# A hybrid conv and attention layer on one core: the last pair's sums in SBUF, one weight half on VectorE, and four steps moved in time

## The chip, the core and the metric

The kernel runs on one core of one Trainium2 chip. The metric is device microseconds of that core for one execution. The engines are TensorE (PE, with weight loads shown apart as PEld), VectorE (DVE), ScalarE (ACT), GpSimd (POOL) and SyncE (SP, which here issues DMAs only). ACT also issues a few DMAs (its queue is shown as ACTq).

## The reference

S = D = 1024, all in float32. A decoder layer with two branches from one projection:

```
mod = c @ w_ada + b_ada;  shift, scale, gate = split(mod, 3)
h = rmsnorm(x, norm_g) * (1 + scale) + shift
glu_a, glu_b, z_conv, q, k, v, z_att, g_conv, g_att = split(h @ w_in)
u = causal_conv31(glu_a * sigmoid(glu_b)) + conv_b
y_conv = (silu(layernorm(u, conv_ln_g, conv_ln_b)) * silu(z_conv)) @ w_conv_out
att = dilated causal window attention, 3 groups of 8 heads of 64, rope on q and k
y_att = (att * silu(z_att)) @ w_att_out
merged = sigmoid(g_conv) * y_conv + sigmoid(g_att) * y_att
out = rmsnorm(x + gate * (merged @ w_o)) * final_g
```

## The kernel before

**Arithmetic.** A float32 operand is split in a high part (rounded to the type that TensorE takes at full rate, fp32r) and a low part (the rest), and each product is three matmuls: high by high, low by high, high by low (L73 to L75, L616, L276). ACT makes a high half by a copy (`whi`, L57, L462), POOL or DVE the low one by a subtraction (`wlo`, L58, L465). Names: `hh` and `hl` are the halves of h (with the channels on the partitions), `wraw` a weight tile as loaded, `d` a PSUM bank.

**Start.** The first products are those of the values. They run on x times a gain before the full h is known. For the first of eight channel tiles the gain column comes from a modulation product on DVE (L171, L298); then `gained_high(0, half)` (L240, on ACT) makes the high part of x, `v_high(0, half)` (L250, on ACT) that of the weights, and DVE makes the second half of x (L301). PE's first matmuls (L276) take both. Later `scaled(kt)` (L355 to L362) makes h of a channel tile: DVE multiplies by the row of root mean squares (L359), ACT writes the high part and the full h (L361), SP stores it. In the loop at L391 DVE makes the low part of h (L393) and, by `shift(kt)`, the shift column of a later tile (L171, L174).

**The planned stage** (from L426). Units of matmuls are steps; `at(step, rank, fn)` hangs the other engines' work onto a step, by rank (EARLY, COPY, EVICT, HIGH, POST and so on), and what is hung at a step is written out around that step's matmuls. `Raw(step, source)` is a weight load at a step, `Form` its split into halves, `Gated` the eviction of a product with its gate. The layer norm of the conv branch sums squares on DVE (`tot`, L801, L805), then sixteen 1-wide matmuls (L130) turn the totals into column sums, eight small DVE and ACT operations make the scales (`lcols`, L113 to L136), and PE transposes those (L821). Just then PE works on the values: groups of twelve matmuls (L616). The conv branch's output weights (`w_co`, eight tiles) are loaded by `output(step, d)`; each output tile multiplies by a loaded gate (`sgc`, L924), is stored to `cscr` (L930), and a column of the output gate is computed beside it (`gate_sum`, its weights `wada`, L937, by DVE at L171). The columns go to `gscr` (L1115). All these transfers are issued by SP in program order, and an instruction that waits on SP holds those behind it.

**Attention.** Slots of half a projection unit each (from −11) carry a hand-written order for PE, DVE, ACT and SP. POOL is not in it: its order is set by the framework's scheduler. `out_combos(k)`, k = 0 to 3, loads two tiles of `w_o` (`oc`, L1549), combines them by four POOL operations (L1552, L1553, L1555, L1556) and stores them to `tscr` (L1559); its four parts are hung on four slots. POOL also makes the low halves (L58) of the projection's weights. `move_kq` (L1287) moves finished keys and queries (`kqp`) between partitions by DMA; the scores (L1357) read them as `k`, `q` and `ql`. Slot 0 has the first scores.

**The end.** Pairs of row tiles t1 and t2 come out of `merged @ w_o` in four accumulations. For the last pair `last_part(t, n, ps, first)` (L1842 to L1847) multiplies a half of 512 columns by the gate, adds the residual, takes the sum of squares on ACT and multiplies by `final_g`; `out_norm` gives total, root (on ACT) and refinement of the inverse root, and `both_rows` (L1959 to L1970) scales the two tiles and stores them.

Of the kernel before, what the change touches and what calls it, by code (L numbers as in the profile page):

```python
# [8 lines left out]
F32 = mybir.dt.float32  # L9
F32R = mybir.dt.float32r  # L10
I32 = mybir.dt.int32
AF = mybir.ActivationFunctionType
# [4 lines left out]
P = 128  # L17
S = 1024
D = 1024
KT = 8  # L20
# [19 lines left out]
def layer(ctx: ExitStack, tc: tile.TileContext, a, out):  # L40
    nc = tc.nc
# [134 lines left out]
    with sbuf_pool("start") as st, tc.manual_schedule(  # L176
# [6 lines left out]
        wa_t, v_raw, u_raw = {}, [], []  # L183
# [62 lines left out]
        def shift(kt):  # L246
            modulation(kt, scol[:, kt:kt + 1], wa_t[kt], wa_t[kt], cb)

        def v_high(kp, c=slice(0, 1024)):
            nc.scalar.activation(wv[kp][0][:, c], v_raw[kp][:, c], AF.Copy)  # L250
# [46 lines left out]
        nc.vector.tensor_add(gcol[:, 0:1], gcol[:, 0:1], scol[:, 0:1])  # L297
        nc.vector.tensor_scalar(gcol[:, 0:1], gcol[:, 0:1], one_b[:, 0:1], ng[:, 0:1], op0=add, op1=mult)  # L298
        gained_high(0, halves[0])
        v_high(0, halves[0])  # L300
        nc.vector.tensor_scalar(hh[:, 0, halves[1]], x_t[0][:, halves[1]], gcol[:, 0:1], None, op0=mult)  # L301
        nc.scalar.activation(cb[:, halves[0]], spread, AF.Copy)
        v_high(0, halves[1])
        v_low(0, halves[0])
# [41 lines left out]
        def u_low(i):  # L346
            hi, lo = u_w[i]
            nc.vector.tensor_sub(lo, u_raw[i], hi.bitcast(F32))
# [43 lines left out]
        for kt in range(KT):  # L392
            nc.vector.tensor_sub(hl[:, kt], h_of[kt], hh[:, kt].bitcast(F32))  # L393
            if kt == 0:
                u_low(2)
            if kt + 2 < KT:
                scaled(kt + 2)
            if kt + 3 < KT:
                shift(kt + 3)
            if kt == 6:  # L400
                shift_parts(slice(0, KT))
            c = slice(kt * P, (kt + 1) * P)
            for i, (wh, wl) in enumerate(u_w):
                if i == 2 and kt == 7:
                    p_row = bank()[0:2]
                    shift_row(p_row, slice(0, KT))
                for half in range(2):
                    s = slice(half * 512, half * 512 + 512)
                    mm3(first[2 * i + half], wh[:, c], wl[:, c], hh[:, kt, s], hl[:, kt, s], kt == 0, kt == KT - 1)
# [35 lines left out]
    def at(step, rank, fn):  # L445
        todo.setdefault(step, []).append((rank, len(todo[step]), fn))
# [83 lines left out]
        (nc.gpsimd if c else nc.vector).tensor_sub(t_lo[i, c], t_raw[i, c], t_hi[i, c].bitcast(F32))  # L530

    behind = []
    credit = [0.0]
    now = [0]
    taps_done = [-1]
# [67 lines left out]
    def values(step, g, turn):  # L603
        ps = []
        raws = [Raw(step + 2 * kp - 7, a["w_v"][g, kp]) for kp in range(4)]
        forms = [Form(step + k, raws[k // 2].half(k % 2)) for k in range(KT)]

        def group(k):
            def fn():
                for i in range(4):  # L610
                    t = 4 * turn + i
                    c = slice(t * P, t * P + P)
                    if k == 0:
                        ps.append(bank())
                    for n, (l, r) in enumerate(((hh, forms[k].hi), (hh, forms[k].lo), (hl, forms[k].hi))):
                        nc.tensor.matmul(ps[i], l[:, k, c], r, start=k == 0 and n == 0, stop=k == KT - 1 and n == 2)  # L616
                if k == KT - 1:
                    for i in range(4):
                        at(now[0], EVICT, lambda i=i: out(i))
            return fn  # L620

        def out(i):
            t = 4 * turn + i
            vs = piece("gs", "gs", 4)
            nc.scalar.activation(vs, ps[i], AF.Copy)
            nc.sync.dma_start(vscr[t * P:t * P + P, g * 512:(g + 1) * 512], vs)
        return [group(k) for k in range(KT)]
# [162 lines left out]
    def norm_squares():  # L790
        pm = row_of_mean[0]
        v_loads((KT - 1,))
        tot2 = slot("n2", "tot2")
        last = None
        for ct in range(KT):
            nc.vector.scalar_tensor_tensor(vt[ct], pm, -1.0 / D, vt[ct], op0=mult, op1=add)
            yield TAP
            sq = conv_in("sq")[:, 0:S] if ct else tot2
            nc.scalar.activation(sq, vt[ct], AF.Square)
            if last is not None:  # L800
                nc.vector.tensor_add(tot2, tot2, last)  # L801
                yield TAP
            last = sq if ct else None
        nc.scalar.activation(one_b[:, 0:1], ones[:, 0:1], AF.Sqrt)
        nc.vector.tensor_add(tot2, tot2, last)  # L805
        yield TAP

        def sums():
            pc = bank()[:, 0:8]
            col_sums(pc, tot2)  # L810
            at(now[0], POST_, lambda: scales(pc))
        at(now[0] + 1, EARLY, sums)

    def scales(pc):
        lcols = rstd_cols(pc, "l")
# [164 lines left out]
        return [group(k) for k in range(KT)]  # L980

    def output(step, d):
        raw = Raw(step - 6, a["w_co"][d])
        forms = [Form(step + 2 * i, raw.half(i)) for i in range(2)]
        out = Gated(step, d)
        ps = {}

        def group(i, half):
            def fn():
                if i == 0:  # L990
                    ps[half] = bank()
                block(ps[half], forms[i], u_block(i, half), i == 0, i == 1)
                if i:
                    at(now[0], POST_, lambda: out.out(half, ps[half]))
            return fn
        return [group(i, half) for i in range(2) for half in range(2)]
# [546 lines left out]
    def out_combos(k):  # L1543
        if not spare:
            spare.extend(ap_.tile([P, S], F32, name="oc", tag="oc", bufs=4) for _ in range(4))
        t = [x.rearrange("p (n c) -> p n c", n=2) for x in (spare[2:] if k else spare[:2])]
        o = slice(k % 2 * 512, k % 2 * 512 + 512)
        for i in range(2):
            nc.sync.dma_start(t[i], a["w_o"][:, 2 * i + k // 2, :, o].rearrange("n p c -> p n c"))  # L1549
        yield  # L1550
        (b11, b12), (b21, b22) = ((x[:, 0], x[:, 1]) for x in t)
        nc.gpsimd.tensor_sub(b11, b11, b12)  # L1552
        nc.gpsimd.tensor_sub(b12, b12, b22)  # L1553
        yield
        nc.gpsimd.tensor_add(b22, b22, b11)  # L1555
        nc.gpsimd.tensor_sub(b21, b21, b22)  # L1556
        yield
        for i in range(2):
            nc.sync.dma_start(tscr[k // 2][1 - i][:, :, o].rearrange("n p c -> p n c"), t[i])  # L1559
        yield  # L1560
# [9 lines left out]
    def in_steps(it, slots):  # L1570
        for x in slots:
            beside.setdefault(x, []).append(it)
# [9 lines left out]
                  (110, w_out(0, 2)), (111, first_ao()), (113, w_out(0, 3))):  # L1582
        in_steps(it, [x, x + 2])
    for k in range(4):
        in_steps(out_combos(k), [(-9, -6, 2, 10)[k] + x for x in (0, 3, 4, 5)])
    raw_for(0)
    prepare(0)
    stream = pieces()
# [69 lines left out]
    def cols_of(half):  # L1658
        return slice(half * 512, half * 512 + 512)
# [151 lines left out]
    def out_norm(step, t, halves):  # L1811
# [27 lines left out]
        at(step + 1, EVICT, root)  # L1839
        at(step + 1, POST_, scaled)  # L1840

    def last_part(t, n, ps, first):  # L1842
        c = cols_of(n)
        nc.vector.tensor_mul(ps, first, rows_of["gate_b"][:, c])
        nc.vector.tensor_add(ps, ps, xs[t][:, c])
        nc.scalar.activation(late["sy"][:, 512:1024], ps, AF.Square, accum_out=sums_[t][:, n:n + 1])
        nc.vector.tensor_mul(xs[t][:, c], ps, rows_of["fg_b"][:, c])  # L1847

    def b_block(n, kh):
        def rhs(k):  # L1850
# [91 lines left out]
    def out_end(p, box, t1, t2):  # L1942
        n11, ns1, ns2, n12, ns3, ns4, n22 = slots_of[p]
        gate2 = cols_of(1)
        steps = {}

        def shared():
            g = box["g"]
            nc.vector.tensor_mul(g, g, rows_of["gate_b"][:, gate2])
            nc.vector.tensor_add(xs[t1][:, gate2], g, xs[t1][:, gate2])  # L1950
            nc.vector.tensor_sub(xs[t2][:, gate2], xs[t2][:, gate2], g)

        def first_row():
            last_part(t1, 1, box["b"], box["b"])
            steps[t1] = out_norm(0, t1, None)
            for fn in steps[t1][:2]:
                fn()

        def both_rows():  # L1959
            last_part(t2, 0, box["d"], box["d"])  # L1960
            steps[t2] = out_norm(0, t2, None)
            for fn in steps[t2][:2]:
                fn()
            steps[t1][2]()
            nc.scalar.activation(xs[t1], xs[t1], AF.Copy, scale=steps[t1][3])
            nc.scalar.dma_start(out[t1 * P:t1 * P + P], xs[t1])
            steps[t2][2]()
            nc.vector.tensor_scalar(xs[t2], xs[t2], steps[t2][3], None, op0=mult)
            for n in range(2):
                nc.sync.dma_start(out[t2 * P:t2 * P + P, cols_of(n)], xs[t2][:, cols_of(n)])  # L1970

        at(ns1 + 1, POST_, shared)
        at(n12, POST_, lambda: last_part(t1, 0, box["a"], box["a"]))
        at(ns3, POST_, lambda: last_part(t2, 1, box["g"], box["d"]))
        at(ns4, POST_, first_row)
        at(n22, POST_, both_rows)
# [71 lines left out]
```

## Time and profile before

| | us |
|---|---|
| three runs | 1195.22, 1197.32, 1197.81 |
| median | 1197.32 |
| the profiled execution | 1197.42 |
| its span | 1195.6 |
| PE busy | 1178.0 |
| DVE busy | 912.0 |
| ACT busy | 604.1 |
| POOL busy | 537.0 |

The span is the time from the first to the last instruction of the profiled execution; its granted TensorE clock was 0.996 of full. A row of the timeline gives the start (us from the span's start), the duration, the engine, the kernel's line, the operation, output and inputs by name, and their shapes. In brackets stands how long the engine was idle before it, and what ended that. A busy PE is one that has matmuls in its pipe: its rows overlap, since a matmul starts before the one ahead has ended.

### The profile page before, as it was taken

How to read it: one execution, taken by the hardware profiler on the slowest of the kernel's cores; microseconds unless marked ns; L12 is line 12 of the kernel's file. 1: busy time of each engine (PE TensorE's matmuls, PEld its weight loads, DVE VectorE, ACT ScalarE, POOL GpSimd, SP SyncE). 2: the span in 40 equal slices, each digit the busy share in tenths (PEclk: the TensorE clock that was granted, in tenths of full speed). 3: DMA queues.
4: the chain of work that ended last, by engine and by line, in shares of the span. 5: the costliest groups of instructions: out<-in, count | busy, mean ns of one | idle time of the engine just before them, and what ended most of it. 6: DMA issues, size and time to landing. Idle time of an engine off the chain costs nothing.

```text
span 1195.6 us, 17343 instructions
## 1 busy us (share of the span) xinstructions
PE 1178.0 (99%) x5970; PEld 983.7 (82%) x5970; DVE 912.0 (76%) x1465; ACT 604.1 (51%) x1245; POOL 537.0 (45%) x389
## 2 busy tenths in 40 slices
PE   9999999999999999999999999999999999999996
PEld 7877888888888888778878888888888888888884
DVE  7979999999999998897357657877877773455576
ACT  5764344544445344841116656566666655336543
POOL 0005878788787774672463311111111022117882
PEclk9999999999999999999999999999999999999998
DMA  9684332222324147746788765565576574679341
GB/s 356 218 299 162 124 105 106 106 74 94 121 83 141 62 141 281 252 165 236 193 226 237 201 176 137 169 182 141 164 192 148 134 195 133 195 242 368 123 141 70
DMA packets 105213, 206.01 MB, mean 172 GB/s; under 512 B 29923, under 2 KB 43555, under 8 KB 105126
## 3 DMA queue, kind: packets, MB, share of 16 engines
q1 hardware_dynamic: 88304, 197.78, 52.6%
q10 hardware_dynamic: 16822, 7.14, 2.1%
q8 instruction: 47, 0.77, 0.3%
q14 instruction: 40, 0.33, 0.1%
HBM read 129.59 MB, written 43.82 MB: 145 GB/s over the span
## 4 chain that ended last, share of the span: by engine, by line
PE 85%; DVE 5%; ACT 3%; DMA 3%; issue 1%; SPq 1%; POOL 1%; ACTq 0%; DVEq 0%; POOLq 0%
PE d L75 22%; PE d L73 22%; PE d L74 22%; PE o L1394 4%; PE d L616 4%; PE d L276 3%; PE s L1357 3%; PE t L1373 3%; DMA wraw<-in_w_v 1%; ACT d L845 1%; DVE tot L801 1%; SPq L1287 0%; DMA gcscr<-gs 0%; ACT uh L861 0%; DMA wraw<-in_w_co 0%
## 5 line engine op out<-in xcount | busy, mean ns | idle before, releaser
L558 DVE SCALAR_TENSOR_TENSOR acc<-u,cw,acc 128x1024 f32<-128x1024 f32 x232 | 298.8, 1288 | 6.6
L73 PE MATMUL d<-hh,whi 128*128 128x512 f32 x752 | 294.9, 392 | 0.0
L74 PE MATMUL d<-hl,whi 128*128 128x512 f32 x752 | 293.6, 390 | 0.5 <-DVE hl L393 0.5
L75 PE MATMUL d<-hh,wlo 128*128 128x512 f32 x752 | 293.3, 390 | 0.0
L465 POOL TENSOR_TENSOR wlo<-wraw,whi 128x512 fp32r<-128x512 f32 x130 | 175.9, 1362 | 211.1 <-ACT whi L462 210.9
L58 POOL TENSOR_TENSOR wlo<-wraw,whi 128x512 fp32r<-128x512 f32 (+1 forms) x56 | 86.3, 1558 | 325.8 <-ACT whi L57 325.8
L75 PEld LDWEIGHTS d<-hh,wlo 128*128 128x128 f32 x752 | 141.2, 188 | 30.0
L74 PEld LDWEIGHTS d<-hl,whi 128*128 128x128 f32 x752 | 141.3, 188 | 27.4 <-DVE hl L393 1.3
L73 PEld LDWEIGHTS d<-hh,whi 128*128 128x128 f32 x752 | 141.4, 188 | 26.4
L462 ACT ACTIVATE whi<-wraw 128x512 fp32r<-128x512 f32 x130 | 79.2, 624 | 103.7 <-DMA wraw<-in_w_co 51.1
L1366 ACT ACTIVATE sb<-sb,stats 128x128 f32<-128x128 f32 (+1 forms) x192 | 84.7, 443 | 36.2 <-DVE stats L1362 36.0
L1362 DVE CUSTOM_DVE_ANT_0 sb<-s,mask 128x128 f32<-128x128 f32 (+1 forms) x192 | 59.7, 349 | 40.5 <-PE s L1357 37.7
L1373 PE MATMUL t<-ident,sb 128*128 128x128 f32 x280 | 73.9, 277 | 0.1
L1394 PE MATMUL o<-ph,vt 128*64 128x128 f32 (+1 forms) x432 | 66.0, 253 | 0.0
L1191 DVE TENSOR_TENSOR pl<-t,ph 128x384 fp32r<-128x384 f32 (+2 forms) x96 | 52.1, 543 | 14.7 <-ACT ph L1188 13.9
L1188 ACT ACTIVATE ph<-t 128x384 fp32r<-128x384 f32 (+2 forms) x96 | 45.4, 473 | 31.5 <-PE t L1373 20.1
L1188 ACT ACTIVATE kqp<-rot 128x512 fp32r<-128x512 f32 x24 | 23.2, 966 | 67.2 <-DVE rot L1211 41.6
L1357 PE MATMUL s<-k,ql 128*128 128x128 f32 (+1 forms) x192 | 55.1, 292 | 0.1
L1394 PE MATMUL o<-pl,vt 128*64 128x128 f32 (+1 forms) x216 | 52.8, 261 | 0.0
L1357 PE MATMUL s<-k,q 128*128 128x128 f32 (+1 forms) x192 | 51.2, 272 | 0.9 <-DMA ql<-kqp 0.9
L616 PE MATMUL d<-whi,hh 128*128 128x512 f32 x128 | 50.4, 394 | 0.0
L1394 PEld LDWEIGHTS o<-ph,vt 128*64 128x64 f32 x432 | 48.3, 136 | 2.3
(358 smaller groups left out, 2733.0 us busy)
## 6 DMA issues: line engine op xcount, KB each, us to landing
wraw<-in_w_t SPq DMA_DIRECT2D x67, 512.0 KB, 4.3
k<-kqp SPq DMA_DIRECT2D x96, 128.0 KB, 2.7
q<-kqp SPq DMA_DIRECT2D x96, 128.0 KB, 2.4
wraw<-in_w_v SPq DMA_DIRECT2D x19, 512.0 KB, 3.8
wa<-in_w_ada SPq DMA_DIRECT2D x16, 512.0 KB, 6.3
ql<-kqp SPq DMA_DIRECT2D x48, 128.0 KB, 2.4
wg<-wscr SPq DMA_DIRECT2D x48, 128.0 KB, 3.0
hscr<-x SPq DMA_DIRECT2D x8, 512.0 KB, 3.5
```

Of the source, the lines that this page charges most:

```text
L58: (lo_eng or nc.vector).tensor_sub(lo, raw, hi.bitcast(F32))
L73: nc.tensor.matmul(ps, lh, rh, start=start, stop=False, skip_group_check=again)
L74: nc.tensor.matmul(ps, lh, rl, start=False, stop=False, skip_group_check=again)
L75: nc.tensor.matmul(ps, ll, rh, start=False, stop=stop, skip_group_check=again)
L462: nc.scalar.activation(self.hi, src(), AF.Copy)
L465: nc.gpsimd.tensor_sub(self.lo, src(), self.hi.bitcast(F32))
L558: nc.vector.scalar_tensor_tensor(acc, u[:, k:k + S], cw[:, ct, k:k + 1], acc, op0=mult, op1=add)
L616: nc.tensor.matmul(ps[i], l[:, k, c], r, start=k == 0 and n == 0, stop=k == KT - 1 and n == 2)
L1357: products.append((w, lambda c=c, w=w, l=x[:, ts_], r=k[:, ks], i=i: nc.tensor.matmul(ps[:, c:c + w], l, r, start=i == 0, stop=i == 1)))
L1366: nc.scalar.activation(sb[:, c:c + w], sb[:, c:c + w], AF.Exp, bias=stats[:, t, h, 1:2], scale=-1.0, accum_out=stats[:, t, h, 0:1])
L1373: yield from ((lambda c=c: nc.tensor.transpose(ps[:, c:c + P], sb[:, c:c + P], ident)) for c in range(0, o, P))
L1394: nc.tensor.matmul(out_, l, r, **kw))
```

## The change

Six edits:

1. At the start the first half of the first weight tile's high part is copied by DVE instead of ACT, and the second half of x's high part is made by ACT instead of DVE.
2. In the loop over channel tiles `shift` comes one turn later and stands ahead of `scaled` instead of behind it.
3. The column sums go from the start of a step to the middle of a group of values: the function is put on a list, and the group takes it after six of its twelve matmuls.
4. The raw loads of `output` stand two steps earlier.
5. The first two `out_combos` begin at slots −11 and −9 instead of −9 and −6.
6. For the last pair the sum goes to SBUF (`xs`), where the square and the final multiply read it; the product goes to a tile of its own (`yt`). In `both_rows` the first tile is finished and stored (by SP) ahead of the second one's last part, and the second tile's two stores go by SP and ACT.

```
-        v_high(0, halves[0])
-        nc.vector.tensor_scalar(hh[:, 0, halves[1]], x_t[0][:, halves[1]], gcol[:, 0:1], None, op0=mult)
+        nc.vector.tensor_copy(wv[0][0][:, halves[0]], v_raw[0][:, halves[0]])
+        gained_high(0, halves[1])
...
+            elif kt + 2 < KT:
+                shift(kt + 2)
             if kt + 2 < KT:
                 scaled(kt + 2)
-            if kt + 3 < KT:
-                shift(kt + 3)
...
+                    if i == 1 and middle:
+                        middle.pop()()
...
-        at(now[0] + 1, EARLY, sums)
+        at(now[0] + 1, EARLY, lambda: middle.append(sums))
...
-        raw = Raw(step - 6, a["w_co"][d])
+        raw = Raw(step - 8, a["w_co"][d])
...
-        in_steps(out_combos(k), [(-9, -6, 2, 10)[k] + x for x in (0, 3, 4, 5)])
+        in_steps(out_combos(k), [(-11, -9, 2, 10)[k] + x for x in (0, 3, 4, 5)])
...
         nc.vector.tensor_mul(ps, first, rows_of["gate_b"][:, c])
-        nc.vector.tensor_add(ps, ps, xs[t][:, c])
-        nc.scalar.activation(late["sy"][:, 512:1024], ps, AF.Square, accum_out=sums_[t][:, n:n + 1])
-        nc.vector.tensor_mul(xs[t][:, c], ps, rows_of["fg_b"][:, c])
+        nc.vector.tensor_add(xs[t][:, c], ps, xs[t][:, c])
+        nc.scalar.activation(late["sy"][:, 512:1024], xs[t][:, c], AF.Square, accum_out=sums_[t][:, n:n + 1])
+        nc.vector.tensor_mul(done_[t][:, c], xs[t][:, c], rows_of["fg_b"][:, c])
...
         def both_rows():
+            steps[t1][2]()
+            nc.scalar.activation(done_[t1], done_[t1], AF.Copy, scale=steps[t1][3])
+            nc.sync.dma_start(out[t1 * P:t1 * P + P], done_[t1])
             last_part(t2, 0, box["d"], box["d"])
             steps[t2] = out_norm(0, t2, None)
-            for fn in steps[t2][:2]:
+            for fn in steps[t2][:3]:
                 fn()
-            steps[t1][2]()
-            nc.scalar.activation(xs[t1], xs[t1], AF.Copy, scale=steps[t1][3])
-            nc.scalar.dma_start(out[t1 * P:t1 * P + P], xs[t1])
-            steps[t2][2]()
-            nc.vector.tensor_scalar(xs[t2], xs[t2], steps[t2][3], None, op0=mult)
-            for n in range(2):
-                nc.sync.dma_start(out[t2 * P:t2 * P + P, cols_of(n)], xs[t2][:, cols_of(n)])
+            nc.vector.tensor_scalar(done_[t2], done_[t2], steps[t2][3], None, op0=mult)
+            for n, eng in enumerate((nc.sync, nc.scalar)):
+                eng.dma_start(out[t2 * P:t2 * P + P, cols_of(n)], done_[t2][:, cols_of(n)])
```

Lines of the changed kernel stand up to seven further down. POOL at the start of attention, before (`oc` are the `w_o` tiles, L58 the low halves of the projection's weights; "x4" is four in a row):

```order
L1552 TENSOR_TENSOR oc<-oc 128x512
L1151 MEMSET mask_4755 64x64
L1553 TENSOR_TENSOR oc<-oc 128x512
L1555 TENSOR_TENSOR oc<-oc 128x512
L1556 TENSOR_TENSOR oc<-oc 128x512
L58 TENSOR_TENSOR wlo<-wraw,whi 128x8x64 x4
L1552 TENSOR_TENSOR oc<-oc 128x512
L1553 TENSOR_TENSOR oc<-oc 128x512
L1555 TENSOR_TENSOR oc<-oc 128x512
L1556 TENSOR_TENSOR oc<-oc 128x512
L58 TENSOR_TENSOR wlo<-wraw,whi 128x8x64 x2
```

And in the changed kernel at the same place:

```order
L1555 TENSOR_TENSOR oc<-oc 128x512
L1154 MEMSET mask_4755 64x64
L1556 TENSOR_TENSOR oc<-oc 128x512
L1558 TENSOR_TENSOR oc<-oc 128x512
L1559 TENSOR_TENSOR oc<-oc 128x512
L1555 TENSOR_TENSOR oc<-oc 128x512
L1556 TENSOR_TENSOR oc<-oc 128x512
L1558 TENSOR_TENSOR oc<-oc 128x512
L1559 TENSOR_TENSOR oc<-oc 128x512
L58 TENSOR_TENSOR wlo<-wraw,whi 128x8x64 x6
```

The four operations of k = 1 have moved ahead of four of L58, the low halves of two projection units.

DVE at the end of the program, before, from the third part of the last pair on (`xt` is a row tile, `r` and `tmp` the columns of the inverse root):

```order
L1847 TENSOR_TENSOR xt<-d,fg_b 128x512
L1818 TENSOR_SCALAR r<-ss 128x1
L1819 TENSOR_SCALAR r<-r 128x1
L1844 TENSOR_TENSOR d<-d,gate_b 128x512
L1845 TENSOR_TENSOR d<-d,xt 128x512
L1847 TENSOR_TENSOR xt<-d,fg_b 128x512
L1818 TENSOR_SCALAR r<-ss 128x1
L1819 TENSOR_SCALAR r<-r 128x1
L1825 RECIPROCAL tmp_11222<-tmp_11222 128x1
L1826 TENSOR_SCALAR tmp_11222<-tmp_11222,r 128x1
L1827 TENSOR_SCALAR tmp_11222<-tmp_11222 128x1
L1828 TENSOR_SCALAR r<-tmp_11222 128x1
```

The same in the changed kernel:

```order
L1854 TENSOR_TENSOR yt<-xt,fg_b 128x512
L1821 TENSOR_SCALAR r<-ss 128x1
L1822 TENSOR_SCALAR r<-r 128x1
L1828 RECIPROCAL tmp_11224<-tmp_11224 128x1
L1829 TENSOR_SCALAR tmp_11224<-tmp_11224,r 128x1
L1830 TENSOR_SCALAR tmp_11224<-tmp_11224 128x1
L1831 TENSOR_SCALAR r<-tmp_11224 128x1
L1851 TENSOR_TENSOR d<-d,gate_b 128x512
L1852 TENSOR_TENSOR xt<-d,xt 128x512
L1854 TENSOR_TENSOR yt<-xt,fg_b 128x512
L1821 TENSOR_SCALAR r<-ss 128x1
L1822 TENSOR_SCALAR r<-r 128x1
```

The first tile's refinement (four operations on a column) has moved ahead of the second tile's last part.

More of the change, by code (lines that the diff above doesn't have):

```diff
@@ L532, in layer @@
     behind = []
+    middle = []
     credit = [0.0]
@@ L1840, in out_norm @@
         at(step + 1, POST_, scaled)
+    done_ = {}
     def last_part(t, n, ps, first):
         c = cols_of(n)
+        if t not in done_:
+            done_[t] = stk.tile([P, S], F32, name="yt", tag=f"l{t // 4}")
         nc.vector.tensor_mul(ps, first, rows_of["gate_b"][:, c])
-        nc.vector.tensor_add(ps, ps, xs[t][:, c])
-        nc.scalar.activation(late["sy"][:, 512:1024], ps, AF.Square, accum_out=sums_[t][:, n:n + 1])
-        nc.vector.tensor_mul(xs[t][:, c], ps, rows_of["fg_b"][:, c])
+        nc.vector.tensor_add(xs[t][:, c], ps, xs[t][:, c])
+        nc.scalar.activation(late["sy"][:, 512:1024], xs[t][:, c], AF.Square, accum_out=sums_[t][:, n:n + 1])
+        nc.vector.tensor_mul(done_[t][:, c], xs[t][:, c], rows_of["fg_b"][:, c])
     def b_block(n, kh):
```

## The prediction

> **What bounds the kernel now.** I read the page's head and busy times first, then the busy time by windows, PE's waits, and last the timelines of each place that the change touches.
>
> ```profile
> span 1195.6 us, 17343 instructions
> PE 1178.0 (99%) x5970; PEld 983.7 (82%) x5970; DVE 912.0 (76%) x1465; ACT 604.1 (51%) x1245; POOL 537.0 (45%) x389
> ...
> 640.00:1170.00 530.00, 530.00 (x3114) 455.44 (x3113) 348.20 (x861) 310.21 (x786) 160.00 (x108) 1.00 0.62 178
> ...
> 1180.84 0.39 PE L75 MATMUL d<-oh,wf 128*128 128x512 f32 x1
> 1183.56 0.39 PE L75 MATMUL d<-hh,wf 128*128 128x512 f32 x1
> ```
>
> The profiled execution took 1197.42 us: 1195.6 of span and 1.82 around it. It stands 0.10 above the median of the three runs, 1197.32; sums are made against 1197.42. TensorE is busy 99% of the span, and from 640 to 1170 it is busy for all 530.00 of 530 us (first number after the window). The last two rows are matmuls twelve apart near the end: one starts each 2.72 / 12 = 0.227 us, whatever its own 0.39 says. The change removes no matmul, so it can only win where PE stands still: 1195.6 − 1178.0 = 17.6 us in all, of which the start and the tail after the last matmul are most. What remains are single stalls, each with its own releaser. So I go place by place and price PE's idle time there. "Same" below means within 0.2%, 2.4 us, about what a measurement of this kernel can tell from no change.
>
> **The change part by part.**
>
> **Start.** Timeline rows are: start, duration, engine, line, operation, shapes, count, and in brackets the idle time before it with what ended it. The last line is the landing time of the weight loads `wraw`.
>
> ```profile
> 2.13 0.43 SPq L208 DMA_DIRECT2D wraw<-in_w_v  x1
> 8.06 0.72 ACT L240 ACTIVATE hh<-x,gcol 128x512 fp32r<-128x512 f32 x1 [4.36 <-DVE gcol L298]
> 8.69 0.61 ACT L250 ACTIVATE wh<-wraw 128x512 fp32r<-128x512 f32 x1
> 9.35 1.89 PE L276 MATMUL d<-wh,hh 128*128 128x512 f32 x7 [0.60 <-ACT wh L250]
> 11.36 1.22 DVE L171 CUSTOM_DVE_ANT_0 wa<-wa,cb 128x1024 f32<-128x1024 f32 x1
> ...
> DMA to landing us min/median/max: 5.8/6.0/6.1
> ```
>
> ACT makes the high half of x and then the high half of the first weights, and PE waits for the second. The weights landed at 2.13 + 6.1 = 8.2, so a copy on DVE, idle since it made `gcol`, can run at 8.3 to 8.8 beside ACT's 8.06 to 8.78; PE starts near 8.85 instead of 9.35. The second half of x takes the slot on ACT that the weight half had (0.61), so ACT's later work stays. What is next late is the modulation column at 11.36, a chain on DVE that also begins about 0.45 earlier if its load has landed. Minus 0.45, from 0 (that load decides) to −0.55.
>
> **Shift row one turn later.**
>
> ```profile
> 59.26 1.24 ACT L361 ACTIVATE x<-xr,scol,gcol 128x1024 f32<-128x1024 f32 x1
> 60.52 1.23 DVE L393 TENSOR_TENSOR hl<-x,hh 128x1024 fp32r<-128x1024 f32 x1
> 61.80 0.50 PE L74 MATMUL d<-hl,whi 128*128 128x512 f32 x1 [0.54 <-DVE hl L393]
> ```
>
> PE waits 0.54 for `hl`, which looks like DVE being busy with the shift before it. But `hl` needs x from ACT, which ends at 59.26 + 1.24 = 60.50, and `hl` starts at 60.52. Taking the 1.22 us shift out of its way leaves it there: 0, at most −0.08. The last rows come about one shift, 1.2 to 1.5 us, later; nobody waits for those in the trace.
>
> **Column sums.**
>
> ```profile
> 489.08 1.95 PE L130 MATMUL d<-ones,tot 128*128 128x1 f32 x16 [0.76 <-DVE tot L805]
> 492.36 0.17 DVE L119 TENSOR_TENSOR lcols<-ltmp 128x8 f32<-128x8 f32 x1
> 493.70 1.03 PE L821 MATMUL lrow<-ident,lcols 128*128 128x128 f32 x8
> ```
>
> The sixteen small products wait 0.76 for DVE's total. Six 512-wide matmuls now stand ahead of them; at 0.227 they are 1.36 in all, and cover the wait. So the products begin about 489.53 instead of 489.08. Their columns are ready 492.36 + 0.17 − 489.08 = 3.45 later, at 492.98, while PE, with the other six behind the products, would be at the transposes (L821) near 492.7. A new wait of 0.3 takes the place of part of the old one; L821 starts at 493.1 instead of 493.70. Minus 0.6 (−0.3 to −0.9).
>
> **Weight loads of the conv output two steps earlier.**
>
> ```profile
> 545.81 0.46 SPq L924 DMA_DIRECT2D sgc<-gcscr  x1
> 554.34 0.40 SPq L62 DMA_DIRECT2D wraw<-in_w_co  x1
> 561.32 0.50 PE L75 MATMUL d<-uh,wlo 128*128 128x512 f32 x1 [0.53 <-POOL wlo L465]
> ```
>
> The load issued at 554.34 stood in SP's queue behind stores that wait for DVE; ACT and POOL split it late, and PE waits 0.53 (0.69 with the late start of the next matmul). Now it follows the `sgc` load at 545.81, 8 us earlier, far more than is missing. Minus 0.7 (0 to −0.7). On SP it stands ahead of a `cscr` store and a `wada` load and delays them by its issue, 0.4, which DVE's waits there hide.
>
> **Output weights: first load two slots earlier, second three.** Rows of DVE, the landing of the `wada` loads (540 to 595), SP, the landing of `gscr`, then POOL, ACT, DVE and PE.
>
> ```profile
> 580.33 1.28 DVE L171 CUSTOM_DVE_ANT_0 wada<-wada,cb 128x1024 f32<-128x1024 f32 x1 [7.32 <-DMA wada<-in_w_ada]
> ...
> DMA to landing us min/median/max: 3.7/4.0/6.1
> ...
> 589.59 0.37 SPq L1115 DMA_DIRECT2D gscr<-gate_c  x1
> ...
> DMA to landing us min/median/max: 11.9/11.9/11.9
> ...
> 603.32 0.95 POOL L1137 MEMSET ql<- 64x1024 f32 x1 [7.77 <-DMA cscr<-gs]
> 605.57 1.30 POOL L1552 TENSOR_TENSOR oc<-oc 128x512 f32<-128x512 f32 x1
> 610.35 1.63 POOL L1556 TENSOR_TENSOR oc<-oc 128x512 f32<-128x512 f32 x1
> 611.94 2.53 POOL L58 TENSOR_TENSOR wlo<-wraw,whi 128x512 fp32r<-128x512 f32 x2
> 615.60 0.60 ACT L1188 ACTIVATE kqp<-d 128x512 fp32r<-128x512 f32 x1 [4.29 <-PE d L75]
> 616.23 0.69 DVE L1191 TENSOR_TENSOR kqp<-d,kqp 128x512 fp32r<-128x512 f32 x1 [4.20 <-ACT kqp L1188]
> 627.37 0.30 PE L1357 MATMUL s<-k,q 128*128 128x128 f32 x1 [0.92 <-DMA ql<-kqp]
> ```
>
> This is the edit that can cost. POOL runs in order, and the second pair's four subtractions now stand ahead of the low weight halves (L58) that the next projection unit needs. That projection follows the one whose eviction starts at 615.60, and reads its low half in its third matmul, at about 615.85. With POOL otherwise unmoved, the first pair ends at 611.98, four subtractions at 1.33 take it to 617.3, two of L58 (2.53) to 619.85: PE stands 4.0. In return the wait of 0.92 at 627.37 (1.08 with the late start of the next matmul, as above) is hidden, since its transfers do not move with PE. Net +2.9.
>
> But POOL will not be unmoved. It starts when `cscr` has landed, which comes behind `gscr`: 589.59 + 11.9 = 601.5. `gscr` waits for the last `wada` columns, and the one at 580.33 kept DVE for 7.32 because its load took 6.1 behind weight loads that the edit before this one moves ahead in time. At the median 4.0 that is 2.1 less, and up to 0.8 less for two issues (0.4 each) no longer ahead of it; I take 2.6 (1.5 to 3.4). POOL then starts 2.6 earlier, the stall is 1.4, and 1.08 of it takes the place of the later wait: +0.3. Ends: −1.08 (no stall, later wait gone) and +2.9.
>
> The 1.33 is my choice: a subtraction took 1.30 at 605.57 and 1.63 at 610.35, after DVE began its rotary multiplies; at 1.63 four would take 1.2 more, and this term would be +1.5. The Trainium skill, page "SBUF — State Buffer", section "SBUF: two separate sides", says that VectorE and GpSimd share a port pair as an exclusive lock, which a VectorE operation takes when both its inputs are in SBUF, so that a GpSimd operation beside it waits it out. By that rule the second pair, beside operations like that at 616.23 whose `d` is in PSUM, runs at the shorter time. The two POOL rows agree with it, and the longer one would stand only if DVE's rotary work moved beside the second pair.
>
> **Tail.** Rows of DVE and SP, then the landings of the last two stores (L1970) and of the earlier stores of the same size (L1835).
>
> ```profile
> 1178.91 0.69 DVE L1847 TENSOR_TENSOR xt<-d,fg_b 128x512 f32<-128x512 f32 x1 [0.81 <-ACT s4y L1846]
> 1185.52 0.69 DVE L1844 TENSOR_TENSOR d<-d,gate_b 128x512 f32<-128x512 f32 x1
> 1186.24 0.70 DVE L1845 TENSOR_TENSOR d<-d,xt 128x512 f32<-128x512 f32 x1
> 1188.37 0.20 DVE L1818 TENSOR_SCALAR r<-ss 128x1 f32<-128x1 f32 x1
> 1190.42 0.75 DVE L1968 TENSOR_SCALAR xt<-xt,r 128x1024 f32<-128x1024 f32 x1
> 1191.20 1.07 SPq L1970 DMA_DIRECT2D out<-xt  x2
> ...
> DMA to landing us min/median/max: 2.9/3.1/3.2
> ...
> DMA to landing us min/median/max: 2.0/2.1/3.1
> ```
>
> PE is done at 1183.56 + 0.39 = 1183.95 and the span ends at 1195.6; all of that is path. Each of four parts has the 0.81 us in which the final multiply waits for ACT's square, since both read the same PSUM bank. With the sum in SBUF and the product in a tile of its own both read at once, and the wait goes. The first two waits buy little: the third part needs the bank of the matmul at 1180.84 and starts at 1181.3. Its sum is ready 1.42 later (1185.52 to 1186.94 in the fourth), square and accumulation take the 0.81 of the old wait, its total, root and refinement some 1.65, all now ahead of the fourth part, which starts at 1185.17 against 1185.52: −0.35. Its total no longer stands behind the waiting multiply (1188.37 before, 1187.4 now: 0.62 more), and the first tile's refinement is no longer between its root and its scale (0.39 of the 2.05 from 1188.37 to 1190.42). The scale starts at 1189.06, 1.36 earlier. Then the stores: two queues instead of two issues in a row saves 0.35, and the first tile's 512 KB left 3 us before instead of 0.4, so the landing should be nearer the 2.1 of lone stores than the 3.1: 0.8. In all −2.5 (−1.7 if the landing stays at 3.1, −2.9 at best).
>
> **Sum.** −0.45 + 0 − 0.6 − 0.7 + 0.3 − 2.5 = −3.95, so 1197.42 − 3.95 = **1193.5**, 0.33% faster.
>
> **The rivals.**
> A: POOL isn't earlier, because `cscr` or the output weights, not `gscr`, set its start. The stall is 4.0, the term +2.9 instead of +0.3: 1196.1, same. For it: I infer the order of landings from one wait.
> B: The tail keeps its waits, because the sum's write to SBUF and the square stay in series with the fourth part behind the first tile's chain, so only the split stores count: −0.5 instead of −2.5, 1195.5, same. For it: the fourth part now stands behind a root that goes through ACT. Against it: the rows above give that chain its place.
> C: POOL gets far enough ahead (over 4 us) to have no stall, and the wait at 627.37 is hidden as well or filled: 1192.1, faster.
> D, slower: the transfers become the bound at the start of attention. Two more 512 KB loads now stand ahead of the projection's weights.
>
> ```profile
> DMA packets 105213, 206.01 MB, mean 172 GB/s; under 512 B 29923, under 2 KB 43555, under 8 KB 105126
> ```
>
> If what follows `gscr` (0.5 MB of `cscr`, 2 MB of output weights) moved at the span's mean 172 GB/s, it would need 14.5 us from 601.5, to 616.0; four subtractions and L58 then end at 623.9, PE stands 8.0, and the term is +6.9: 1200.1. It decides once the second pair's loads land after POOL is through with the first (609 to 612). Against it: 1.5 MB went between 601.5 and the first subtraction at 605.57, about 370 GB/s, by which the next 1 MB lands by 608.4.
> That the change doesn't do what it says is only possible for the shift, priced at 0.
>
> **How the numbers follow.** Forecast 0.60, A 0.17, B 0.10, C 0.08, D 0.05. Range 1191.3 to 1196.9: the low end is C with the best ends of the tail (0.4), the sums (0.3) and the start (0.1), the high end is A with the tail's worst end (0.8); D is left out with the corners. Faster by over 0.2% (under 1194.9): C, and of the forecast all but a twentieth, where several terms fall short together, with a tenth of B: 0.66. Slower: D and a mishap more, 0.06. Same: 0.28.
>
> **What would show it.** In the profile after: PE's first matmul at 8.8 to 8.9; the 0.54 at 61.8 still there; no wait ahead of the sixteen products but one of about 0.3 ahead of the transposes; no wait for POOL's low halves near 561; one of 1 to 2 us near 614, with the second pair's subtractions ahead of it and no wait near 627; no wait of the last multiplies for the square, and the last stores issued about 1189.8. It is wrong if the stall near 614 is above 3, or the stores leave after 1191.

## The result, and the profile after

The changed kernel took 1203.01 us (median of six runs, 1201.84 to 1203.56) against 1197.12 for the kernel before in the same session: a ratio of 1.005, 95% interval 1.0037 to 1.0063. It is slower by 0.5%; 1193.5 was forecast, with a range up to 1196.9. The profiled execution took 1203.56, of which 1201.8 is span, 6.2 more than before.

The page's head of the changed kernel, its busy times, and PE's waits (microseconds in all, how often, the longest):

```profile
span 1201.8 us, 17347 instructions
PE 1180.8 (98%) x5970; PEld 985.4 (82%) x5970; DVE 913.2 (76%) x1465; ACT 605.5 (50%) x1245; POOL 537.6 (45%) x389
...
PE d L73 <- DVE kqp L1194: 4.4, 1, 4.4
PE d L75 <- POOL wlo L58: 3.2, 1, 3.2
...
PE d L75 <- POOL hh L1688: 0.6, 1, 0.6
PE d L966 <- POOL wlo L465: 0.5, 1, 0.5
PE d L74 <- DVE hl L393: 0.5, 1, 0.5
```

The waits for the column totals, for the first weights and for the first scores are gone. Two new ones, 4.4 and 3.2, are larger than all that went. To see where the time went I set the same PE instruction of both traces side by side (starts in us):

| PE instruction | before | after | after − before |
|---|---|---|---|
| first matmul of the values | 9.35 | 8.75 | −0.60 |
| product that waits for `hl` | 61.80 | 61.69 | −0.11 |
| transposes of the layer norm's scales | 493.70 | 492.93 | −0.77 |
| third matmul after the one that waited near 561 | 562.13 | 560.57 | −1.56 |
| first matmul of the second projection unit | 615.40 | 618.42 | +3.02 |
| its third | 615.86 | 622.84 | +6.98 |
| its twelfth | 617.90 | 626.80 | +8.90 |
| first score | 627.37 | 635.18 | +7.81 |
| last matmul | 1183.56 | 1192.04 | +8.48 |
| end of the span | 1195.6 | 1201.8 | +6.2 |

So PE was 1.56 ahead when attention began, lost 10.5 within twelve matmuls, got 1.1 back at the first scores, lost 0.7 later, and the tail gave back 2.3.

The place of the loss, changed kernel; rows of SP, the landing of `gscr`, then ACT, POOL and PE:

```profile
592.27 0.37 SPq L1118 DMA_DIRECT2D gscr<-gate_c  x1
596.58 0.41 SPq L62 DMA_DIRECT2D wraw<-in_w_t  x1
604.45 0.34 SPq L62 DMA_DIRECT2D wraw<-in_w_t  x1
...
DMA to landing us min/median/max: 12.1/12.1/12.1
...
614.38 0.63 ACT L57 ACTIVATE whi<-wraw 128x512 fp32r<-128x512 f32 x1 [4.18 <-DMA wraw<-in_w_t]
616.52 0.63 ACT L57 ACTIVATE whi<-wraw 128x512 fp32r<-128x512 f32 x1 [1.52 <-DMA wraw<-in_w_t]
617.06 1.07 ACT L1191 ACTIVATE kqp<-d 128x512 fp32r<-128x512 f32 x2
...
606.32 0.95 POOL L1140 MEMSET ql<- 64x1024 f32 x1 [12.34 <-DMA cscr<-gs]
619.09 1.27 POOL L1559 TENSOR_TENSOR oc<-oc 128x512 f32<-128x512 f32 x1
620.32 2.46 POOL L58 TENSOR_TENSOR wlo<-wraw,whi 128x512 fp32r<-128x512 f32 x2
...
618.42 0.80 PE L73 MATMUL d<-hh,whi 128*128 128x512 f32 x1 [4.42 <-DVE kqp L1194]
622.84 0.80 PE L75 MATMUL d<-hh,wlo 128*128 128x512 f32 x1 [3.20 <-POOL wlo L58]
...
618.00:627.00 9.00, 5.38 (x12) 3.83 (x13) 0.96 (x2) 1.16 (x3) 7.17 (x6) 0.52 1.00 327
```

Read it from the top. The gate store went out at 592.27; before it was 589.59, so it is 2.7 later, where I had put it 2.6 earlier. Of the two weight loads that the second projection unit needs, one went out at 596.58 and the other only at 604.45, which is when the gate store landed (592.27 + 12.1 = 604.4). ACT, in order, waited for the one and then the other (4.18 and 1.52), and behind these stood the evictions of the unit before (617.06). The first of the two went out about when it did before, but landed only at 614.27, 17.7 us later: ahead of it in SP's queue stood the gate store, two `cscr` stores and four `oc` loads, and these landed one after the other from 604.4 to 612.2. PE therefore first had no free bank (4.42), and then no low half of the weights (3.20), since POOL, 3.0 later than before, made the second pair's four subtractions first. The last row is the window in which PE began again: after the window's length stand the busy times of PE, PEld, DVE, ACT and POOL, and then the granted clock, 0.52. The matmuls from 622.84 to 626.42 start 0.43 apart (the first 0.59) instead of 0.227, which cost another 1.9.

The order in SP's queue names the reason for 604.45. With the semaphores that each transfer waits for, the rows are, in the changed kernel,

```
L1118 DMA gscr<-gate_c 128x8x1 [waits DMAHW3_49,DVE_49]
L933 DMA cscr<-gs 128x512 [waits DMAHW4_49,DVE_49]
L933 DMA cscr<-gs 128x512 [waits DMAHW5_49,DVE_49]
L1552 DMA oc<-in_w_o 128x2x512 [waits DMAHW6_49,PE_49]
L1552 DMA oc<-in_w_o 128x2x512 [waits DMAHW7_49,PE_49]
L1552 DMA oc<-in_w_o 128x2x512 [waits DMAHW0_49]
L1552 DMA oc<-in_w_o 128x2x512 [waits DMAHW1_49]
L62 DMA wraw<-in_w_t 128x1024 [waits DMAHW2_49,Pool_49]
L62 DMA wraw<-in_w_t 128x1024 [waits DMAHW3_49,Pool_49]
```

This program's transfers take eight completion semaphores in turn, and each waits until the transfer eight ahead of it has landed. The two loads that the change put in make the second weight load the eighth after the gate store. Before, the two weight loads stood on semaphores 0 and 1 and went out together at 596.14. So the ring accounts for the second load and ACT's second wait; the first and longer wait, 4.18, was for a load that had gone out and landed late behind the gate store.

The tail, changed kernel: DVE, ACT, PE and SP rows, then the landing of the last two stores.

```profile
1189.74 0.70 DVE L1851 TENSOR_TENSOR d<-d,gate_b 128x512 f32<-128x512 f32 x1 [0.40 <-PE d L75]
1193.52 0.69 DVE L1851 TENSOR_TENSOR d<-d,gate_b 128x512 f32<-128x512 f32 x1
1197.40 0.75 DVE L1974 TENSOR_SCALAR yt<-yt,r 128x1024 f32<-128x1024 f32 x1
1191.26 0.63 ACT L1853 ACTIVATE s4y<-xt 128x512 f32<-128x512 f32 x1 [1.84 <-DVE xt L1852]
1192.04 0.39 PE L75 MATMUL d<-hh,wf 128*128 128x512 f32 x1
1198.18 0.33 SPq L1976 DMA_DIRECT2D out<-yt  x1
...
DMA to landing us min/median/max: 2.5/2.6/2.7
```

No final multiply waits for the square any more. From PE's last matmul to the last scale it is 1197.40 − 1192.04 = 5.36 instead of 6.86, and from there to the end of the span 4.4 instead of 5.2.

### The profile page after: what moved, and what is told of

It is laid out like the page before. It is cut to its first block, busy times and chain, and to the rows that moved or that the text cites. A ratio compares the mean times of both kernels' runs of the same rounds, so it can differ in the third digit from the quotient of the medians.

```text
span 1201.8 us, 17347 instructions
## 1 busy us (share of the span) xinstructions
PE 1180.8 (98%) x5970; PEld 985.4 (82%) x5970; DVE 913.2 (76%) x1465; ACT 605.5 (50%) x1245; POOL 537.6 (45%) x389
## 4 chain that ended last, share of the span: by engine, by line
PE 85%; DMA 5%; ACT 3%; DVE 3%; POOL 3%; issue 1%; SPq 1%; ACTq 0%; POOLq 0%; DVEq 0%
PE d L75 22%; PE d L73 22%; PE d L74 22%; PE d L617 7%; PE o L1397 4%; PE s L1360 3%; PE t L1376 2%; PE d L276 2%; DMA cscr<-gs 1%; ACT d L848 1%; DMA x<-in_xT 1%; DMA raws<-in_w_ao 1%; ACT uh L864 0%; DMA wada<-in_w_ada 0%; DMA ng<-in_norm_g 0%
## 5 line engine op out<-in xcount | busy, mean ns | idle before, releaser
L58 POOL TENSOR_TENSOR wlo<-wraw,whi 128x512 fp32r<-128x512 f32 (+1 forms) x56 | 85.3, 1541 | 336.3 <-ACT whi L57 336.3
```

Of the source, the lines that this page charges most:

```text
L58: (lo_eng or nc.vector).tensor_sub(lo, raw, hi.bitcast(F32))
```

## The experiments

The theory after the result: two causes at the start of attention, both hanging on the gate store. POOL does the second pair's subtractions ahead of the weights that PE needs (fifth edit), and the second weight load waits for the gate store, which the fourth edit makes later. Rivals: POOL's order alone; the fourth edit alone; the transfers' volume.

**The tail alone.** The kernel before with the last functions of the changed one (`last_part`, `both_rows`).

> The kernel before with the sixth edit alone (sums in SBUF, reordered last rows, split stores). The theory says that this edit did what was forecast: PE's work ends at the same place, the time from PE's last matmul to the end falls by 2.3, so about 1194.8 against 1197.1. Rival: the gain in the tail seen in the changed kernel comes from the shift of everything before it; then under 1 us here.

1194.43 us (eleven runs) against 1197.34, ratio 0.9977, interval 0.9965 to 0.9988. PE's last matmul starts at 1182.90 and the span ends at 1192.6: 9.7 instead of 12.0, as in the changed kernel (9.8). The sixth edit is worth 2.3 by itself in this stretch, where 2.5 was forecast.

**The fifth edit undone, the fourth undone, the fifth alone.**

```
-        in_steps(out_combos(k), [(-11, -9, 2, 10)[k] + x for x in (0, 3, 4, 5)])
+        in_steps(out_combos(k), [(-9, -6, 2, 10)[k] + x for x in (0, 3, 4, 5)])
```

> The changed kernel with the fifth edit undone (output weights loaded and combined at the old slots). The theory says that this edit carries the loss of about 9 us at the start of attention, but that the earlier weight loads (fourth edit) also push the store of the gate columns 2.7 us later, so that a wait of 2 to 3 us for POOL's low halves is left near 614: about 1195. Rival one, the fifth edit is the only cause and the later gate store is harmless: 1193.3 or less. Rival two, the loss comes from the later gate store alone: 1200 or more, with the big waits still there.

```
-        raw = Raw(step - 8, a["w_co"][d])
+        raw = Raw(step - 6, a["w_co"][d])
```

> The changed kernel with the fourth edit undone (weight loads of the conv output at the old step). The theory says that the gate store goes back to about 589, that all that follows it comes 3 us earlier, and that PE's two waits near 614 shrink from 7.6 together to 2 to 4; the wait of 0.5 near 561 comes back. About 1198 to 1199 against 1203 for the changed kernel. Rival, the fourth edit does not move the gate store: 1203.7.

> The kernel before with the fifth edit alone. The theory says that the second of the two weight loads still waits until the gate store has landed (it is the eighth transfer after it), that PE stands 3 to 5 us at the second projection unit, and that the wait of 0.9 at the first scores goes: 1199 to 1201. Rival, this edit carries all of the loss by itself: 1206. Rival, it is harmless without the fourth: 1196 to 1197.

Measured: without the fifth edit 1196.53 (ratio 0.9988, 0.9977 to 0.9999), without the fourth 1198.92 (1.0009, 0.9997 to 1.002), the fifth alone 1201.86 (1.0041, 1.0027 to 1.0055). PE's waits near 614, one line from each of the three in that order:

```profile
PE d L75 <- POOL wlo L58: 1.4, 1, 1.4
```

```profile
PE d L75 <- POOL wlo L58: 4.1, 1, 4.1
```

```profile
PE d L75 <- POOL wlo L58: 3.3, 1, 3.3
618.00:627.00 9.00, 8.19 (x29) 6.62 (x30) 1.25 (x4) 0.00 (x0) 3.23 (x3) 0.81 0.92 299
```

None of the three has the wait for a free bank. With the fifth edit alone the gate store went out at 588.70 and landed at 600.63. The second weight load went out right behind that, at 600.69, but this was early enough: ACT was not held, and what is left is POOL's order: 3.3, and after it the clock of the last line's window, 0.81, with matmuls 0.43 apart (1.7 more). PE went from 0.53 ahead to 3.61 behind at the first scores, 4.1 in all; the case of an unmoved POOL in the forecast had 2.9, from a wait of 4.0 and no slow matmuls. The median is 0.9 above the 1201 expected at most. Without the fifth edit the later gate store leaves a wait of 1.4; its profiled span, 1192.8, is 2.8 below that of the kernel before, but the median of its runs (1194.06 to 1197.8) only 0.8, and the expected 1195 was missed by 1.5.

**The fourth and fifth edits together, and no other.**

> The kernel before with the fourth and fifth edits and none of the others. The fifth alone took 1201.9. The theory says that the fourth makes the gate store later (591 to 592.5 instead of 588.7), with it the second weight load, which waits until that store has landed, and so adds the wait for a free bank to the wait for POOL: 1204 to 1207. Rival, the two add up as parts, the fourth's gain of 0.7 on top: 1201.

1205.78, ratio 1.0073 (1.006 to 1.0086), by far the slowest. Its gate store, weight loads and waits:

```profile
592.62 0.37 SPq L1115 DMA_DIRECT2D gscr<-gate_c  x1
596.92 0.41 SPq L62 DMA_DIRECT2D wraw<-in_w_t  x1
604.59 0.34 SPq L62 DMA_DIRECT2D wraw<-in_w_t  x1
...
PE d L73 <- DVE kqp L1191: 4.0, 1, 4.0
PE d L75 <- POOL wlo L58: 3.8, 1, 3.8
```

This is the changed kernel's picture with two edits of six. The two do not add up as parts: the fourth, with which PE has no wait near 561, costs 3.9 when the fifth is there (1205.78 against 1201.86). In the profiled executions of the eight kernels that have the store at its old place it goes out at 590.48, 590.56, 592.27 and 592.62 with the fourth edit, and at 588.54, 588.70, 589.43 and 589.59 without it, though PE is further on with it (at 562 it is 1.29 to 1.56 ahead of the kernel before, against 0 to 1.04).

**The weights ahead of the second pair's loads.**

```
-        in_steps(out_combos(k), [(-11, -9, 2, 10)[k] + x for x in (0, 3, 4, 5)])
+        in_steps(out_combos(k), [(-11, -8, 2, 10)[k] + x for x in ((0, 2, 3, 4) if k == 1 else (0, 3, 4, 5))])
```

> The changed kernel with the second out_combos begun at slot -8 instead of -9, so that its two loads stand behind the two weight loads in SP's queue and not ahead of them; two of its four POOL operations still stand ahead of the low halves. The theory of two causes says: the weight loads are issued together before 598 and land as before, so the wait for a free bank (4.4 near 614) goes; what is left is POOL, which starts near 605, does six subtractions and the low halves by 617, a wait of 1 to 3. About 1197 to 1199. Rival, POOL's order alone made both waits: 1201 or more, since the waits stay in sum above 5.

1200.69 (1.0026, 1.0009 to 1.0043) with a wide spread, 1197.64 to 1203.96; the time is above what was expected of the theory, and by the time alone the theory and its rival can't be told apart. The trace, that of the fastest of the eight executions, can tell them apart:

```profile
594.57 0.42 SPq L62 DMA_DIRECT2D wraw<-in_w_t  x1
595.08 0.38 SPq L62 DMA_DIRECT2D wraw<-in_w_t  x1
595.51 1.08 SPq L1552 DMA_DIRECT2D oc<-in_w_o  x1
602.95 0.38 SPq L1552 DMA_DIRECT2D oc<-in_w_o  x1
...
PE d L75 <- POOL wlo L58: 3.9, 1, 3.9
```

The weights went out together, the wait for a bank is gone, and the transfer that now stands eighth after the gate store, the last `oc` load, is the one that went out at its landing (602.95). POOL's order still costs 3.9, more than the 1 to 3 expected.

**The gate store moved away.** It goes to slot 96, some 100 us ahead of its reader, once with all six edits and once with the fifth undone.

```
-    nc.sync.dma_start(gscr.rearrange("o (d p) -> p (o d)", p=P), gate_c)
...
+    def gate_out():
+        nc.sync.dma_start(gscr.rearrange("o (d p) -> p (o d)", p=P), gate_c)
+        yield
...
+    in_steps(gate_out(), [96])
```

> The changed kernel with the store of the gate columns moved from the start of attention to slot 96, far later and long before its reader. The theory says that this store, whose tiny packets hold everything behind it for 12 us, is what both causes hang on: without it POOL starts some 6 us or more earlier (near 600), the weights land by 605, and both waits near 614 go, the wait at the first scores too: 1191 to 1192.5. Rival, the transfers take their time by their volume alone: the waits shrink by less than half and it stays above 1198.

> The changed kernel with the fifth edit undone and the gate store at slot 96. The theory says that POOL's order no longer matters and the wait of 1.4 near 614 that was left without the fifth edit goes, while the wait at the first scores (0.9) may come back, as the loads of the second output weights stand ahead of its transfers: 1192 to 1193.5. Rival: no difference from the kernel with the fifth edit undone alone, 1196.5.

1194.0 (0.9973, 0.9964 to 0.9982) and 1193.37 (0.9967, 0.9956 to 0.9979). With all six edits, POOL's start and three of the second pair's operations, a rotary operation of DVE, and PE's wait there are

```profile
597.45 0.95 POOL L1139 MEMSET ql<- 64x1024 f32 x1 [3.38 <-DMA cscr<-gs]
606.59 1.74 POOL L1554 TENSOR_TENSOR oc<-oc 128x512 f32<-128x512 f32 x1
608.41 1.63 POOL L1555 TENSOR_TENSOR oc<-oc 128x512 f32<-128x512 f32 x1
610.11 1.29 POOL L1557 TENSOR_TENSOR oc<-oc 128x512 f32<-128x512 f32 x1
...
605.51 1.66 DVE L1213 TENSOR_TENSOR rot<-rot,sh 128x512 f32<-128x512 f32 x1
...
PE d L75 <- POOL wlo L58: 0.8, 1, 0.8
```

The same edits as in the changed kernel, the same bytes, and 9.0 us less: POOL starts at 597.45 instead of 606.32, the wait for a bank is gone and 0.8 is left of the one for POOL. It is not the volume. Expected were 1191 to 1192.5: these 0.8 were not. They are the size of what the second pair's first two operations took longer, 1.74 and 1.63 where the third took 1.29: being earlier, they now lie beside DVE's rotary work, which was slowed as well (1.66; the same operation took 0.69 in the kernel before where POOL was idle). That is the port lock of the Trainium skill's page "SBUF — State Buffer", section "SBUF: two separate sides", in the very case that the prediction left open; in the changed kernel the second pair ran beside no such operation, at 1.27 to 1.28. And the fifth edit, which was to pay by taking away the wait at the first scores, is worth nothing here: without it that wait is 0.2.

**Which edits are worth something then.** The late gate store and the tail, with and without the column sums and weight loads, and with the first two edits besides.

> The kernel with the gate store late and the fifth edit undone (1193.4), and now the first and second edits undone too; left are the column sums, the earlier weight loads and the tail. The theory says that the first two edits bring nothing that lasts: PE starts 0.4 to 0.6 later but stands at the same place by 50 us, so no difference, 1193 to 1194. Rival: the start's 0.45 lasts as forecast; then 0.4 to 0.6 slower than with them.

> The kernel before with the sixth edit and the late gate store alone. The theory says that the column sums and the earlier weight loads are worth 0.65 and 0.75 at their places when nothing behind takes them back, so that without them it is 1194.5 to 1195. Rival: the late gate store gains nothing by itself beyond the tail alone (1194.4), and the other two nothing either: all three the same.

> The kernel of the eighth run once more beside the two others on one chip, for the comparison: 1193.4, by the theory 0.0 to 0.5 from the one without the first two edits and 1.2 to 1.6 faster than the one with the tail and the late gate store alone.

On one chip, against 1197.49 for the kernel before: 1192.71 (0.9964, 0.9952 to 0.9976) without the first two edits, 1193.83 (0.9972, 0.996 to 0.9983) with only the tail and the late store, 1192.24 (0.9966, 0.9954 to 0.9978) with all but the fifth. Sums and weight loads bring 1.1 to 1.6 at the medians, about the 1.2 to 1.6 expected, though all three kernels were faster than expected, the one with only the tail and the late store by 0.7. In the one profiled execution of that kernel PE had no wait near 561 even without the fourth edit, so the traces do not show that the weight loads bring their part. The first two edits bring nothing that these runs can tell (0.5, in spreads of 2). All three beat the kernel before and, by their medians, the changed one.

## Why the prediction was wrong, by its own steps

**Start: −0.45 forecast, nothing that lasts.** PE's first matmul was at 8.75, as said, but by 61.7 only 0.11 was left. The chain on DVE that was to begin earlier met its load:

```profile
10.94 1.23 DVE L171 CUSTOM_DVE_ANT_0 wa<-wa,cb 128x1024 f32<-128x1024 f32 x1 [0.29 <-DMA wa<-in_w_ada]
```

That was the lower bound of this term. Kernels without the edit vary as much by themselves: 8.90 to 9.41 for the first matmul, and 55.98 to 56.78 for the first product with the full h, against 56.05 to 56.60 in those with it.

**Shift: 0, right.** The wait for `hl` at 61.69 is 0.50 where it was 0.54.

**Column sums: −0.6, right.** −0.66 by the table; the sixteen products started at 489.45 without a wait (489.53 forecast) and the transposes at 492.93 (493.1). But the wait that it removes is not in every kernel without the edit: it is 0.76 in the kernel before, 0.45 with the tail and the late store, 0.29 with the fourth and fifth edits, and not there with the tail alone or the fifth edit alone.

**Weight loads: −0.7 at their place, right, but what they do behind it was the wrong sign.** The wait near 561 went and PE gained 0.79. Of five kernels without the edit three have this wait (0.53 to 0.62) and two have none, so a part of this may be chance. The step that failed is the next: "the one at 580.33 kept DVE for 7.32 because its load took 6.1 behind weight loads that the edit before this one moves ahead in time", from which I took a gate store 2.6 earlier. It came 2.7 later. In the changed kernel the wait that stood at 580.33 is there still, 6.36 at 582.32, and each earlier `wada` product is late too (541.0, 551.0, 559.1, 564.8, 573.3 against 540.4, 550.3, 557.7, 563.0, 570.4). The weight loads did go out earlier (570.20 to 571.6, some 5 us ahead of that `wada` load), and the load still took 5.9, so standing right behind them was not what made it long. It was issued 2.1 later.

That the fourth edit is the cause is shown by the four and four kernels above, and by the two pairs among them that differ in that edit alone: 588.70 against 592.62, and 589.43 against 592.27. The traces show what it does. POOL's subtractions for `w_co` come earlier and now lie beside DVE's `wada` products and the additions behind them, which the forecast had no term for. DVE and POOL, first in the changed kernel, then at the same product with the fourth edit undone:

```profile
564.83 1.92 DVE L171 CUSTOM_DVE_ANT_0 wada<-wada,cb 128x1024 f32<-128x1024 f32 x1 [1.74 <-DMA wada<-in_w_ada]
566.78 1.12 DVE L174 TENSOR_TENSOR gate_c<-gate_c,bada 128x1 f32<-128x1 f32 x1
...
564.37 3.52 POOL L465 TENSOR_TENSOR wlo<-wraw,whi 128x512 fp32r<-128x512 f32 x2 [2.87 <-ACT whi L462]
...
562.69 1.22 DVE L171 CUSTOM_DVE_ANT_0 wada<-wada,cb 128x1024 f32<-128x1024 f32 x1 [0.71 <-DMA wada<-in_w_ada]
563.96 0.16 DVE L174 TENSOR_TENSOR gate_c<-gate_c,bada 128x1 f32<-128x1 f32 x1
...
561.02 1.51 POOL L465 TENSOR_TENSOR wlo<-wraw,whi 128x512 fp32r<-128x512 f32 x1 [0.19 <-ACT whi L462]
566.81 1.29 POOL L465 TENSOR_TENSOR wlo<-wraw,whi 128x512 fp32r<-128x512 f32 x1 [4.28 <-ACT whi L462]
```

Beside POOL the product took 1.92 instead of 1.22 and the addition of a column 1.12 instead of 0.16. In the same two traces the additions at 553.34 and 560.40 took 1.26 and 1.12 instead of 0.16, and the product at 582.32 took 1.99 instead of 1.23. The delay then goes from tile to tile: DVE's multiply stands behind the product, a `cscr` store waits for the multiply, and SP issues the next `wada` load behind that store. The `wada` load of 565.39 went out at 568.91. That these longer operations make up all of the 2.7 is not shown.

**Output weights: +0.3 forecast, +9.4 measured** (from −1.56 to +7.81). Three things were missed. POOL's start was 3.0 later instead of 2.6 earlier, behind the gate store. Both weight loads hung on that store: the first landed behind it in the queue, and the second was issued only when it had landed, which the order of the queue with its semaphores would have told. Rival D had late transfers, but by volume at 172 GB/s: the 2.6 MB behind the store landed within 7.9 us of it, some 330 GB/s, and with the store moved away the same bytes left no wait for a bank. And ACT, in order, carried that lateness to the evictions and so to PE's banks. Then each wait was priced at its own length, without the 1.5 to 2.5 of slow matmuls that follow a long one: with the fifth edit alone the wait was 3.3, less than the 4.0 forecast for an unmoved POOL, and yet PE lost 4.1 where 2.9 was forecast. The wait at the first scores went, as forecast (1.1).

**Tail: −2.5, measured −2.3.** The scale came 1.50 earlier instead of 1.36, the stores gave 0.78 instead of 1.15 since they landed in 2.6 and not 2.1. Inside, the third part waits for PE's bank, as said (0.40, then 1189.74, 2.30 ahead of the last matmul), and the fourth begins 1.48 behind that matmul where it was 1.96, 0.48 earlier (0.35 forecast).

**What stays open.** In the last stage PE lost another 0.7, with a wait of 0.56 for POOL's `hh` at 1083.77. None of the other kernels has that wait (the one with the fourth edit undone has 1.0 for POOL's `wf` instead); its cause was not tried. From the first scores to the last matmul the kernels differ from the one before by anything from 0.8 less to 1.0 more, so it need not belong to the change.

The sum by steps: −0.1 − 0.7 − 0.8 + 9.4 + 0.7 − 2.3 = +6.2, the span's difference.

## What to carry to other kernels

When a step is moved in a transfer queue, look not only at bytes and buffers but at what each transfer waits for: in this program's ring of eight completion semaphores one slow transfer holds whichever comes a ring's length behind it, and two more loads in between change which one that is; those issued in between landed behind it too. A slow transfer of tiny pieces next to a tight stage is worth moving first; here that alone turned a loss of 0.5% into a gain of 0.3%. Next to the tail alone (1194.43 without it, 1193.83 with it, on two chips) no gain is shown. And a gain at a place that hangs on a chain through three engines has no sign until the chain is followed link by link.

## What the runs showed of the hardware

After a wait of 3.2 to 4.4 PE's granted clock was down, and the next 7 to 13 matmuls of 512 columns started 0.43 apart (the first up to 0.59) instead of 0.227, 1.5 to 2.5 us more in five kernels; after waits of 0.8 and 1.4 there was no such stretch (granted clock 1.00 in the windows from 618 to 627). A wait is not needed for it, though. With the fifth edit alone there is one more such stretch, where PE did not wait: behind the sixteen 1-wide matmuls of the column totals, from 489.84 to 493.25, the granted clock was 0.50 (third number from the end), and nine matmuls cost 1.7 more.

```profile
487.78 1.95 PE L130 MATMUL d<-ones,tot 128*128 128x1 f32 x16
...
489.84:493.25 3.41, 3.41 (x9) 2.63 (x9) 0.96 (x6) 2.73 (x5) 1.21 (x2) 0.50 1.02 380
```

No other kernel here has a slow stretch at that place, so no length of wait is shown to be a threshold. The Trainium skill's page "TensorE: Matmul & The Clock Gate", in its Part 1, says that an idle window of about 3.4 us puts the array to half its clock, and a busy one of that length brings it back. The 0.50 over 3.41 us agrees with it. An estimate from the page's figure, half of 3.4 us, would have put 1.7 on top of each such wait.

The gate store, 4 KB in single words, took 11.7 to 12.4 us to land in eight kernels (13.8 to 14.5 at slot 96, in five). At its old place the `cscr` stores issued behind it landed 0.6 to 2.2 us after it; with the store at slot 96 the same stores landed 2.0 to 2.6 us after their own issue.
